# A state-space layer in a hybrid trunk: decay matrices in place, row copies by head group, rows requested two pairs ahead, first exponentials and first group's order tied

## The chip, the cores and the metric

The kernel runs on one core of one Trainium2 chip. The metric is the device time of one execution in microseconds. The program contains two layers of an encoder: three sub-layers each, of which one, the bidirectional state-space mixer, is touched by the change. Everything is computed in float32; the large projections split each operand into a high and a low part and use three products.

## The reference, cut to what matters

The mixer projects the 512 x 1024 input to z, x, B, C and dt, puts x, B and C through a short convolution and SiLU, and then runs one scan forward and one backward over 32 heads of 64 channels. Heads come in four groups of eight that share B and C (128 states). One direction is, chunk by chunk:

```python
a = (dt * A)                                   # per head and position
a_cs = cumsum(a)
L = exp(segsum(a))                             # decay from s to l, lower triangle
CB = einsum('bclgn,bcsgn->bgcls', Cc, Bc)      # shared by the heads of a group
y_diag = einsum('bgcls,bgjcls,bcsgjp->bclgjp', CB, L, Xc)
states = einsum('bclgn,bgjcl,bclgjp->bcgjpn', Bc, decay_states, Xc)
y_off = einsum('bclgn,bcgjpn,bgjcl->bclgjp', Cc, states, exp(a_cs))
y = y_f + y_b + X * d_skip                     # then SiLU(z), grouped RMS norm, w_out
```

So for each head there is a matrix of decays, exp(cumulated sum at l minus that at s), masked to a triangle, times C·B, times X. The kernel works with two chunks of 256 positions instead of four of 128.

## The kernel before, in words

**Who does what.** TensorE does projections, transposes and the products of the scan. ScalarE (ACT) does exponentials, SiLU, evictions of PSUM and the high halves of weights (L123). VectorE (DVE) does the low halves (L124), convolution taps (L743, L746), and elementwise products. GpSimd (POOL) masks the decay rows (L844) and adds the two masked halves (L858). All DMAs of this stage are asked for on SyncE's queue (SP), in one order.

**The rows.** `dt_chain` computes dt, the log decays and their cumulated sums, position on partitions, 64 columns for each of four blocks of 128 positions (32 heads forward, 32 backward). It transposes them (L720) to 64 rows of 512, one per head and direction, and evicts them as `rows` (L722) and, as exponentials, `rowe` (L724, L725). Four DMAs (L729) write both to DRAM as `scr`, 16 copies of every row, 3 MB together. A head's decay rows come back broadcast over 128 partitions: `rw` (forward and backward row, 512 KB, L827) and `ch` (exponential row, 256 KB, L829). Both are asked for in `ssd_head`, on demand, with two `rw` and three `ch` buffers.

**The matrices.** `ssd_head` multiplies ch by C (L830) and masks: two masks in place on rw, two into `dx`. `ssd_mats` makes, per head and chunk c, a matrix E (one of five buffers): two exponentials of 256 columns into E (L852, L853), two of 128 in dx (L854, L855), one add on GpSimd on the two diagonal blocks (L858), one product with C·B (`cb`) on VectorE (L859). The bias of each exponential is a column of `bias`, one per head. `ssd_out` then does the six products of a pair of heads (two heads side by side, 64 output rows each; L869): two with X transposed (`xt`), one with the carried state and ch.

**Groups and half pairs.** The loop at L929 goes over four groups, and within a group over eight steps s: four pairs of heads, two chunks each. A step is a half pair. Between the products of the steps stand the units of a list `todo`: projections of the next group's B, C and x (six units), of z, and, from the second group on, of the output. In the first group there are eight units. `prepare(g)` transposes B and x of a group, makes `cb`, and returns `sums`, which makes the carried states (L812, L816). At step 0 one unit runs first, and `sums` is kept behind it.

**What sets the order.** A planner takes the program in this order and, with its own costs, fixes for every engine one order of instructions ahead of the run; it may move a ready instruction ahead of one that it thinks is late. Extra edges can be given: `gated`/`shut` keep an instruction behind the last projection, and an edge without a semaphore (NOSYNC) sets only the order within an engine. The conv evictions of later units are already kept behind the last exponentials (`last_exp`, L741). Tiles of 128 x 512 come from one pool of 32 buffers (`big`); PSUM has four `acc`, two `mid` and two `ln` banks.

## Time and profile before

| what | value |
|---|---|
| median of 3 runs | 2158.78 us (2158.37 to 2164.72) |
| the profiled execution's own time | 2159.59 us |
| its span, first to last instruction | 2157.8 us |
| granted TensorE clock | 0.995 |
| TensorE matmul busy | 2111.7 us (98%) |
| VectorE busy | 1766.9 us (82%) |
| ScalarE busy | 1089.3 us (50%) |
| GpSimd busy | 165.0 us (8%) |
| state-space mixer, roughly | 380 to 790 us of the span |
| first group's scan in it, roughly | 439 to 506 us |

A row of the views gives an engine or a line of the kernel, what it writes from what, its count and its times in microseconds; behind an arrow stands what ended the idle time before it. Windows rows give a stretch, its length, and for each engine busy time and count in brackets; at the end stand the granted clock, the DMA engines' busy share and GB/s. Where such a row is filtered to one line of the kernel, only TensorE's two columns (products, weight loads) are left. SPq is SyncE issuing DMAs. A float32 product of the scan shows as two records.

### The profile page before, as it was taken

How to read it: one execution, taken by the hardware profiler on the slowest of the kernel's cores; microseconds unless marked ns; L12 is line 12 of the kernel's file. 1: busy time of each engine (PE TensorE's matmuls, PEld its weight loads, DVE VectorE, ACT ScalarE, POOL GpSimd, SP SyncE). 2: the span in 40 equal slices, each digit the busy share in tenths (PEclk: the TensorE clock that was granted, in tenths of full speed). 3: DMA queues.
4: the chain of work that ended last, by engine and by line, in shares of the span. 5: the costliest groups of instructions: out<-in, count | busy, mean ns of one | idle time of the engine just before them, and what ended most of it. 6: DMA issues, size and time to landing. Idle time of an engine off the chain costs nothing.

```text
span 2157.8 us, 34073 instructions
## 1 busy us (share of the span) xinstructions
PE 2111.7 (98%) x13230; PEld 1859.5 (86%) x13230; DVE 1766.9 (82%) x2924; ACT 1089.3 (50%) x1824; POOL 165.0 (8%) x258
## 2 busy tenths in 40 slices
PE   7999999999999999999999999999999999999997
PEld 6889899866777698999999989899888878989897
DVE  6979998557676888989988988997777878958796
ACT  4424354768656646344456434353866647424343
POOL 0000000045233400000000000000111100000000
PEclk9999999999999999999999999999999999999999
DMA  8863635375444442636443273723322212423231
GB/s 323 303 218 111 231 121 178 99 199 148 149 132 139 123 146 79 237 115 217 145 129 117 90 252 101 256 90 112 99 70 78 89 59 69 137 76 114 75 118 40
DMA packets 90082, 301.19 MB, mean 140 GB/s; under 512 B 10048, under 2 KB 13504, under 8 KB 89920
## 3 DMA queue, kind: packets, MB, share of 16 engines
q1 hardware_dynamic: 88384, 294.81, 41.7%
q0 software_dynamic: 1536, 4.20, 0.9%
q8 instruction: 104, 1.70, 0.3%
q14 instruction: 58, 0.48, 0.1%
HBM read 289.53 MB, written 5.24 MB: 137 GB/s over the span
## 4 chain that ended last, share of the span: by engine, by line
PE 84%; DVE 6%; issue 3%; ACT 3%; DMA 2%; POOL 2%; POOLq 0%; SPq 0%; ACTq 0%; DVEq 0%
PE acc L176 67%; PE mid L176 10%; PE mid L869 1%; DVE raw L195 1%; PE mid L1056 1%; DMA raw<-in_wdn 1%; PE ln L176 1%; POOL E L858 1%; DMA raw<-in_adaw 1%; DMA raw<-in_wgu 1%; ACT wh L123 1%; PE ln L1078 1%; DVE wl L124 1%; DVE wal L116 0%; PE ln L816 0%
## 5 line engine op out<-in xcount | busy, mean ns | idle before, releaser
L176 PE MATMUL acc<-hi,wh 128*128 128x256 f32 (+1 forms) x1568 | 522.1, 334 | 3.2 <-ACT hi L153 2.1
L176 PE MATMUL acc<-lo,wh 128*128 128x256 f32 (+1 forms) x1568 | 521.7, 333 | 0.3 <-DVE lo L154 0.2
L176 PE MATMUL acc<-hi,wl 128*128 128x256 f32 (+1 forms) x1568 | 522.0, 333 | 0.0
L176 PE MATMUL acc<-uh,wh 128*128 128x256 f32 (+1 forms) x1160 | 391.4, 338 | 0.1
L176 PE MATMUL acc<-ul,wh 128*128 128x256 f32 (+1 forms) x1160 | 389.8, 336 | 0.0
L176 PE MATMUL acc<-uh,wl 128*128 128x256 f32 (+1 forms) x1160 | 389.5, 336 | 0.0
L123 ACT ACTIVATE wh<-raw 128x1024 fp32r<-128x1024 f32 (+1 forms) x210 | 213.0, 1021 | 268.5 <-PE acc L176 103.1
L527 ACT ACTIVATE wh<-raw 128x1024 fp32r<-128x1024 f32 x198 | 209.3, 1059 | 250.0 <-DVE raw L537 117.5
L176 PEld LDWEIGHTS acc<-hi,wh 128*128 128x128 f32 x1568 | 296.1, 189 | 37.5 <-ACT hi L153 5.4
L176 PEld LDWEIGHTS acc<-lo,wh 128*128 128x128 f32 x1568 | 296.1, 189 | 30.5 <-DVE lo L154 2.1
L176 PEld LDWEIGHTS acc<-hi,wl 128*128 128x128 f32 x1568 | 296.1, 189 | 29.1
L124 DVE TENSOR_TENSOR wl<-raw,wh 128x1024 fp32r<-128x1024 f32 (+1 forms) x210 | 247.6, 1182 | 55.5 <-ACT wh L123 54.5
L528 DVE TENSOR_TENSOR wl<-raw,wh 128x1024 fp32r<-128x1024 f32 x198 | 241.0, 1219 | 22.0 <-ACT wh L527 21.1
L176 PEld LDWEIGHTS acc<-uh,wh 128*128 128x128 f32 x1160 | 219.4, 189 | 28.9 <-issue 5.9
L176 PEld LDWEIGHTS acc<-ul,wh 128*128 128x128 f32 x1160 | 219.8, 190 | 24.4 <-issue 2.8
L176 PEld LDWEIGHTS acc<-uh,wl 128*128 128x128 f32 x1160 | 219.8, 190 | 23.1 <-issue 1.5
L537 DVE TENSOR_TENSOR raw<-raw 128x512 f32<-128x512 f32 x264 | 181.3, 688 | 5.0 <-DMA raw<-in_wgu 0.2
L195 DVE SCALAR_TENSOR_TENSOR raw<-raw,cond 128x1024 f32<-128x1024 f32 x144 | 174.0, 1219 | 9.8 <-DMA raw<-in_adaw 9.4
L401 DVE SCALAR_TENSOR_TENSOR resid<-acc,gv,resid 128x512 f32<-128x512 f32 (+1 forms) x156 | 104.5, 672 | 69.3 <-PE acc L176 69.0
L341 POOL TENSOR_TENSOR rr<-vr,mhalf 128x2 f32<-128x2 f32 x12 | 9.2, 767 | 1516.5 <-DVE vr L337 1516.5
L176 PE MATMUL mid<-uh,wh 128*128 128x256 f32 (+2 forms) x332 | 99.7, 302 | 0.5 <-DVE up L569 0.5
L176 PE MATMUL mid<-uh,wl 128*128 128x256 f32 (+2 forms) x332 | 99.4, 299 | 0.0
(267 smaller groups left out, 3965.3 us busy)
## 6 DMA issues: line engine op xcount, KB each, us to landing
raw<-in_wgu SPq DMA_DIRECT2D x176, 512.0 KB, 4.0
raw<-in_adaw SPq DMA_DIRECT2D x144, 512.0 KB, 4.7
raw<-in_wdn SPq DMA_DIRECT2D x64, 448.0 KB, 4.0
raw<-in_win SPq DMA_DIRECT2D x40, 512.0 KB, 4.2
raw<-in_wdn SPq DMA_DIRECT2D x32, 512.0 KB, 4.7
rw<-scr SPq DMA_DIRECT2D x32, 512.0 KB, 5.6
ch<-scr SPq DMA_DIRECT2D x32, 256.0 KB, 3.7
raw<-in_wso SPq DMA_DIRECT2D x16, 512.0 KB, 3.6
```

The costliest lines, as they stand in the source:

```text
L123: nc.scalar.activation(hi[:, :n], raw, AF.Copy)
L124: nc.vector.tensor_tensor(out=lo[:, :n], in0=raw, in1=hi[:, :n].bitcast(F32), op=ALU.subtract)
L176: last = nc.tensor.matmul(o, lhsT=a, rhs=b, start=start and j == 0, stop=j == n - 1, skip_group_check=not start)
L195: nc.vector.scalar_tensor_tensor(out=raw, in0=raw, scalar=1.0, in1=cond, op0=ALU.mult, op1=ALU.mult, accum_out=mods[l][:, j : j + 1],)
L401: nc.vector.scalar_tensor_tensor(out=res[d][:, a:b], in0=pd[:, a:b], scalar=gvec[n][:, d : d + 1], in1=res[d][:, a:b], op0=ALU.mult, op1=A ...
L527: nc.scalar.activation(x[0], r, AF.Copy)
L528: nc.vector.tensor_tensor(out=x[1], in0=r, in1=x[0].bitcast(F32), op=ALU.subtract)
L537: nc.vector.tensor_tensor(out=o, in0=x, in1=y, op=ALU.add)
L858: nc.gpsimd.tensor_tensor(out=dg, in0=dg, in1=dx[:, c], op=ALU.add)
L869: nc.tensor.matmul(py[hh * 64 : (hh + 1) * 64, cc], lhsT=lhs, rhs=rhs, start=k == 0, stop=k == 2)
L1056: nc.tensor.matmul(ss[m], lhsT=q[:, c], rhs=qks[h, 1][m], start=j == 0, stop=j == 1)
L1078: gated(nc.tensor.transpose(pw[:, k * P : (k + 1) * P], w[:, k * P : (k + 1) * P], ident))
```

## The change

Heads are reordered in memory so that the eight heads of group g lie at rows g, g+4, ... of 32; `col(h)` finds a head's column. The exponentials are a third block of 32 rows, so one transpose gives 96 rows, and `rowe` goes. `scr` becomes four tensors, one per group, each written by three DMAs in `copy_rows`: group 0 at once, group g+1 at the second pair of group g. The E buffers go: the exponentials, the add and the product with C·B write over `rw`, of which there are six. `fetch` and `fetch_ch` ask for the rows of a pair two pairs ahead. The ch multiplication is done once for both heads. In the first group, the first pair's masks and the exponentials and matrices of its first half are put into `prepare`, between `cb` and `xt`, and the xt evictions are ordered behind the last of these exponentials. In the first group, too, the products of a half pair are kept behind the last projection (`shut`), the following projections behind the products (`hold`), and the units come two at a time after each pair. In all groups the first products of a half pair wait for both heads' matrices (`ready`).

```diff
+                if j == 0 and hold[0] is not None:
+                    tc.add_manual_dep(last.ins, hold[0].ins.name, NOSYNC, reason="behind the state-space products")
...
-        scr = dp.tile([16, 32, 3, T], F32, name="scr")
+        scr = [dp.tile([16, 8, 3, T], F32, name=f"scr{g}") for g in range(NG)]
+        rows = big(name="rows")
...
+            nc.vector.tensor_copy(cs[:, 0:2, 64:96], pc4[:, 0:2, 32:64])
+            nc.vector.tensor_copy(cs[:, 2:4, 64:96], pc4[:, 2:4, 0:32])
             pr = acc("ln")
             for i in range(4):
-                nc.tensor.transpose(pr[:64, i * P : (i + 1) * P], cs[:, i * 64 : (i + 1) * 64], ident)
-            rows = big(name="rows")
+                nc.tensor.transpose(pr[:96, i * P : (i + 1) * P], cs[:, i, :96], ident)
             nc.scalar.activation(rows[:64], pr[:64], AF.Copy)
-            rowe = big(name="rowe")
-            nc.scalar.activation(rowe[32:64, :W], pr[32:64, :W], AF.Exp)
-            nc.scalar.activation(rowe[0:32, W:], pr[0:32, W:], AF.Exp)
+            nc.scalar.activation(rows[64:96], pr[64:96], AF.Exp)
+            copy_rows(0)
...
-            for j, a, b, src in ((0, 0, T, rows[0:32]), (1, 0, T, rows[32:64]), (2, 0, W, rowe[32:64]), (2, W, T, rowe[0:32])):
-                nc.sync.dma_start(
-                    scr[:, :, j, a:b].rearrange("r h x -> h r x"), src[:, a:b].unsqueeze(1).broadcast_to([32, 16, b - a])
-                )
+        def copy_rows(g):
+            for j in range(3):
+                src = rows[j * 32 + g : j * 32 + 32 : 4].unsqueeze(1)
+                nc.sync.dma_start(scr[g][:, :, j].rearrange("r h x -> h r x"), src.broadcast_to([8, 16, T]))
...
+            first = between(cbs) if between else None
             for i in range(4):
...
-                nc.scalar.activation(x, pp, AF.Copy)
+                e = nc.scalar.activation(x, pp, AF.Copy)
+                if first is not None:
+                    tc.add_manual_dep(e.ins, first.ins.name, NOSYNC, reason="decay matrices first")
...
+        def fetch(ft):
+            if ft >= 16:
+                return
+            for h in (2 * ft, 2 * ft + 1):
+                rw = ep.tile([P, 2, T], F32, tag="rw", name="rw", bufs=NRW)
+                nc.sync.dma_start(rw, scr[h // 8][:, h % 8].unsqueeze(1)[:, :, 0:2].broadcast_to([NREP, P // NREP, 2, T]))
+                rows_of[h] = rw
...
+        def fetch_ch(ft):
+            if ft >= 16:
+                return
+            ch = ep.tile([P, 2, T], F32, tag="ch", name="ch")
+            for hh in range(2):
+                src = scr[ft // 4][:, 2 * ft % 8 + hh].unsqueeze(1)[:, :, 2]
+                nc.sync.dma_start(ch[:, hh, :], src.broadcast_to([NREP, P // NREP, T]))
+            ch_of[ft] = ch
+
+        def ssd_heads(ft, Ct):
+            ch = ch_of.pop(ft)
+            nc.vector.tensor_tensor(out=ch, in0=ch, in1=two(Ct), op=ALU.mult)
+            return [ssd_head(2 * ft + hh, ch[:, hh, :]) for hh in range(2)]
...
-            E = ep.tile([P, T], F32, tag="E", name="E", bufs=NE)
...
+            nc.scalar.activation(rw[:, 0, cc], rw[:, 0, cc], AF.Exp, bias=bias[:, i, col(h) : col(h) + 1])
+            nc.scalar.activation(rw[:, 1, cc], rw[:, 1, cc], AF.Exp, bias=bias[:, i + 1, 32 + col(h) : 33 + col(h)])
...
+            ready[c].append(
+                nc.vector.tensor_tensor(out=E, in0=E, in1=cbs[c].rearrange("p (k q) -> p k q", k=2), op=ALU.mult)
+            )
...
+                    m = gated(
+                        nc.tensor.matmul(py[hh * 64 : (hh + 1) * 64, cc], lhsT=lhs, rhs=rhs, start=k == 0, stop=k == 2)
+                    )
+                    for x in ready[c] if k == 0 else ():
+                        tc.add_manual_dep(m.ins, x.ins.name, SYNC, reason="one run of products")
...
+        for k in range(2):
+            fetch(k)
+            fetch_ch(k)
         silu(bc + xs)
...
+        def first_mats(cbs):
+            begun.extend(ssd_heads(0, bc[1]))
+            for hh in range(2):
+                ssd_mats(hh, 0, begun[hh][0], begun[hh][2], cbs)
+            return made[0]
+
+        cur = prepare(0, xs, bc, first_mats)
...
-                    heads = [ssd_head(ft * 2 + hh, Ct) for hh in range(2)]
+                    heads = begun if ft == 0 else ssd_heads(ft, Ct)
+                    if g < NG - 1 and pr_ == 1:
+                        copy_rows(g + 1)
                     py = acc("mid")
-                mats = [ssd_mats(ft * 2 + hh, c, heads[hh][0], heads[hh][2], cbs) for hh in range(2)]
+                for hh in range(2) if s or g else ():
+                    ssd_mats(ft * 2 + hh, c, heads[hh][0], heads[hh][2], cbs)
+                if c == 1:
+                    fetch(ft + 2)
...
-                ssd_out(pr_, c, py, mats, [hd[1] for hd in heads], xt, states)
+                if g == 0:
+                    shut()
+                last_out = ssd_out(pr_, c, heads, py, xt, states)
+                gate[0] = None
+                if c == 1:
+                    fetch_ch(ft + 2)
...
-                while done < (s + 1) * tot // 8:
+                if g == 0:
+                    hold[0] = last_out
+                while done < ((s + 1) // 2 * 2 if g == 0 else s + 1) * tot // 8 + (g == 0 and 0 < s < 7):
                     todo[done]()
                     done += 1
+                hold[0] = None
```

More of the change, by code (lines that the diff above doesn't have):

```diff
@@ L21 @@
 NA = 32
-NE = 5
+NRW = 6
 NG = 4
+NREP = 16
 NST = 128
@@ L160, in split_into @@
             )
-    last_mm, gate = [None], [None]
+    last_mm, gate, hold = [None], [None], [None]
     def gated(x):
@@ L678, in dt_chain @@
                 nc.tensor.transpose(pt[:, i * 64 : (i + 1) * 64], dtT[:64, i * P : (i + 1) * P], ident[:64, :64])
-            e1, e2, e3 = (ep.tile([P, T], F32, tag="E", name="E", bufs=NE) for _ in range(3))
+            e12, e3 = (ep.tile([P, 2, T], F32, tag="rw", name="ew", bufs=NRW) for _ in range(2))
+            e1, e2, e3 = e12[:, 0, :], e12[:, 1, :], e3[:, 0, :]
             v, q, e, uu, lu = e1[:, :W], e1[:, W:], e2[:, :W], e2[:, W:], e3[:, :W]
@@ L776, in silu, with prepare @@
                 tc.add_manual_dep(s.ins, last_in[0].ins.name, SYNC, reason="SiLUs together")
-        def prepare(g, xs, bc):
+        def prepare(g, xs, bc, between=None):
             Bt, Ct = bc
@@ L821, in prepare, with ssd_head @@
             return xt, cbs, states, Ct, sums
-        def ssd_head(h, Ct):
-            src = scr[:, h].unsqueeze(1)
-            rw = ep.tile([P, 2, T], F32, tag="rw", name="rw")
-            nc.sync.dma_start(rw, src[:, :, 0:2].broadcast_to([16, 8, 2, T]))
-            ch = ep.tile([P, T], F32, tag="ch", name="ch", bufs=3)
-            nc.sync.dma_start(ch, src[:, :, 2].broadcast_to([16, 8, T]))
-            nc.vector.tensor_tensor(out=ch, in0=ch, in1=Ct, op=ALU.mult)
+        rows_of = {}
+        def fetch(ft):
[5 more added lines that the diff above has]
+                rows_of[h] = rw
+        ch_of = {}
+        def fetch_ch(ft):
[10 more added lines that the diff above has]
+            return [ssd_head(2 * ft + hh, ch[:, hh, :]) for hh in range(2)]
+        def ssd_head(h, ch):
+            rw = rows_of.pop(h)
             dx = ep.tile([P, 2, 2, P], F32, tag="dx", name="dx")
@@ L849, in ssd_mats @@
         def ssd_mats(h, c, rw, dx, cbs):
[L850 to L855 removed]
+            i, cc = 2 * c, slice(c * W, (c + 1) * W)
@@ L858, in ssd_mats @@
+            dg = rw.rearrange("p d (k q) -> p (d k) q", k=4)[:, i : i + 6 : 5, :]
             nc.gpsimd.tensor_tensor(out=dg, in0=dg, in1=dx[:, c], op=ALU.add)
-            nc.vector.tensor_tensor(out=E, in0=E, in1=cbs[c], op=ALU.mult)
-            return E
-        def ssd_out(pr_, c, py, mats, chs, xt, states):
+            E = rw[:, :, cc]
+            ready[c].append(
+                nc.vector.tensor_tensor(out=E, in0=E, in1=cbs[c].rearrange("p (k q) -> p k q", k=2), op=ALU.mult)
+            )
@@ L863, in ssd_out @@
+        def ssd_out(pr_, c, heads, py, xt, states):
+            col = [slice(pr_ * P + hh * 64, pr_ * P + (hh + 1) * 64) for hh in range(2)]
             cc = slice(c * W, (c + 1) * W)
-            col = [slice(pr_ * P + hh * 64, pr_ * P + (hh + 1) * 64) for hh in range(2)]
             for k in range(3):
                 for hh in range(2):
+                    rw, ch, _ = heads[hh]
                     lhs = xt[2 * c + k][:, col[hh]] if k < 2 else states[1 - c][:, col[hh]]
-                    rhs = mats[hh][:, k * W : (k + 1) * W] if k < 2 else chs[hh][:, cc]
-                    nc.tensor.matmul(py[hh * 64 : (hh + 1) * 64, cc], lhsT=lhs, rhs=rhs, start=k == 0, stop=k == 2)
+                    rhs = rw[:, k, cc] if k < 2 else ch[:, cc]
+                    m = gated(
+                        nc.tensor.matmul(py[hh * 64 : (hh + 1) * 64, cc], lhsT=lhs, rhs=rhs, start=k == 0, stop=k == 2)
+                    )
+                    for x in ready[c] if k == 0 else ():
+                        tc.add_manual_dep(m.ins, x.ins.name, SYNC, reason="one run of products")
+            ready[c].clear()
+            return m
@@ L871, in gated_norm @@
+        ready = [[], []]
         def gated_norm(g, ys, zs, fill=None):
@@ L917, in ssm @@
         run(units_z(0, zs[0])[:2])
-        cur = prepare(0, xs, bc)
+        begun = []
+        def first_mats(cbs):
[4 more added lines that the diff above has]
+        cur = prepare(0, xs, bc, first_mats)
         outs, yrs = {}, {}
@@ L1228, in _layout @@
     A["par"] = par
+    heads = np.arange(32).reshape(4, 8).T.reshape(-1)
+    heads = np.concatenate([heads, heads + 32])
     A["dtp"] = cc(np.concatenate(
-        [rows(np.tile(f[k][0].reshape(-1), 4)) for k in ("ssm_dt_bias", "ssm_a_log")], axis=1
+        [rows(np.tile(f[k][0].reshape(-1)[heads], 4)) for k in ("ssm_dt_bias", "ssm_a_log")], axis=1
     ))
@@ L1256, in _layout @@
     w = f["ssm_w_in"][0]
-    A["wdt"] = cc(w[:, 5120:].reshape(KT, P, 64).transpose(1, 0, 2).reshape(P, 512))
+    A["wdt"] = cc(w[:, 5120:][:, heads].reshape(KT, P, 64).transpose(1, 0, 2).reshape(P, 512))
     b = unit(w[:, :5120])
```

23 lines of the change are left out of this document (12 added, 11 removed).

## The prediction

> **What bounds the kernel now.** I read the page first, then the chain of waits through the state-space layer, then TensorE's own work in stretches of it.
>
> ```profile
> span 2157.8 us, 34073 instructions
> PE 84%; DVE 6%; issue 3%; ACT 3%; DMA 2%; POOL 2%; POOLq 0%; SPq 0%; ACTq 0%; DVEq 0%
> ```
>
> TensorE carries 84% of the chain, so a saving must show as a shorter stretch of TensorE. A busy TensorE proves little: its records overlap, and a product that waits inside the queue still looks busy. So I count instructions. The next rows are the chain in the second head group, where nothing disturbs it.
>
> ```profile
> 532.72 10.93 PE acc L176 x48
> 543.66 1.45 PE mid L869 x12
> ```
>
> Two projections of 24 products are 48 in 10.93 us; the twelve records of one half pair (L869, the state-space products) are 1.45 us, 0.121 each. Now the same two lines over three stretches (length; busy time and count): the first group's from its third half pair's projections on, the quiet one, and the last group's end. The first three rows are L176, the last three L869.
>
> ```profile
> 461.71:506.19 44.48, 30.61 (x119) 21.62 (x119) 1.00 0.76 213
> 532.48:588.33 55.85, 50.35 (x216) 40.13 (x216) 1.00 0.49 151
> 721.49:740.68 19.19, 11.48 (x48) 8.85 (x48) 1.00 0.47 124
> ```
>
> ```profile
> 461.71:506.19 44.48, 12.94 (x74) 5.70 (x72) 1.00 0.76 213
> 532.48:588.33 55.85, 6.06 (x48) 3.09 (x48) 1.00 0.49 151
> 721.49:740.68 19.19, 4.93 (x38) 2.58 (x36) 1.00 0.47 124
> ```
>
> The quiet stretch prices a projection product, the change-overs included: (55.85 - 48 x 0.121) / 216 = 0.232 us. By that the first group's stretch should take 119 x 0.232 + 74 x 0.121 = 36.5 us and takes 44.48: **8.0 us lost**. The last group's end should take 48 x 0.232 + 36 x 0.121 = 15.5 and takes 19.19: **3.7 us lost**. These two are the prize. The clock is 1.00 in all of them, so the loss is order and waits. The chain in the first group shows which:
>
> ```profile
> 442.70 16.33 PE acc L176 x72
> 459.04 2.77 PE mid L869 x24
> 461.80 3.19 DMA ch<-scr
> ...
> 466.75 0.65 PE mid L869 x2
> 467.40 1.13 PE acc L176 x4
> 468.53 1.47 PE mid L869 x10
> ```
>
> Three projections run, then the first pair unbroken. From the second pair on, one head's first product goes out alone (x2), four projection products fall between, then the other ten: the pair is broken up, and the chain goes back to a row transfer before it. GpSimd says how far apart the pairs are (in-place masks, L844, first of each pair):
>
> ```profile
> 473.36 1.14 POOL L844 TENSOR_SCALAR_AFFINE_SELECT rw<-rw 128x256 f32<-128x256 f32 x2 [6.08 <-DMA rw<-scr]
> 483.96 0.77 POOL L844 TENSOR_SCALAR_AFFINE_SELECT rw<-rw 128x256 f32<-128x256 f32 x2 [2.22 <-DMA rw<-scr]
> 494.68 0.80 POOL L844 TENSOR_SCALAR_AFFINE_SELECT rw<-rw 128x256 f32<-128x256 f32 x2 [2.17 <-DMA rw<-scr]
> ```
>
> From 473.36 to 483.96 to 494.68 a pair takes 10.6 and 10.7 us, 2.2 of them waiting for the transfer: about 8.5 us of masks, exponentials, adds and products with C·B per pair.
>
> **Part 1: first group's order fixed (hold, gate, ready).** It adds no instruction; it makes TensorE run two projections, then both half pairs of a pair unbroken, and so on. A pair then needs 10.93 + 2 x 1.45 = 13.8 us of TensorE. The matrices need 8.5 (transfer hidden) to 10.6, so they stay ahead, and the 8.0 us should come back. The bounds are 0 (every pair just late) and 8.0. I take 7.5, near the upper end, because the measured 10.6, wait included, is already below 13.8. The new wait sits on TensorE: behind the first product of a half pair stand all later projections, and behind those ScalarE's conv evictions. The cover is the two projections ahead of each pair.
>
> **Part 2: rows asked for two pairs ahead, matrices in place (NRW = 6, no E).** It removes the five E buffers; the exponentials write over the rows, so the first now waits for all four masks of its head instead of two. Same number of masks, exponentials, adds and products. The multiplication of ch is one instruction of 1024 columns instead of two of 512, on VectorE, hidden. Bytes read back stay the same: 32 times 512 KB and 32 times 256 KB. What moves is the request, past weight loads on SP's queue. What it is worth shows in the last group:
>
> ```profile
> 722.91 1.20 SPq L827 DMA_DIRECT2D rw<-scr  x2
> ...
> 728.55 2.75 POOL L844 TENSOR_SCALAR_AFFINE_SELECT rw<-rw 128x256 f32<-128x256 f32 x2 [3.98 <-DMA rw<-scr]
> ...
> 737.60 0.62 PE L869 MATMUL mid<-E,xt 128*64 128x256 f32 x2 [1.73 <-DVE E L859]
> 739.24 0.86 PE L869 MATMUL mid<-E,xt 128*64 128x256 f32 x5 [1.03 <-DVE E L859]
> ```
>
> The last pair's rows are asked for at 722.91, GpSimd idles 3.98 us for them, and TensorE then waits at 737.60 and 739.24. Asked for two pairs earlier they are there: the masks start some 4 us sooner, which covers 3 of the 3.7 us (between 0, if VectorE is late instead, and 3.7). I take 3.0, and 0.5 more for the last group's first half, whose masks wait the same way. What is late next there is VectorE, whose row stands with the rivals. `fetch_ch` waits for the pair's products and stands on SP ahead of weight loads; the old kernel's ch requests waited there too, and four raw buffers cover it: nothing.
>
> **Part 3: 96 rows, copies per group.** The old four copies move 3 MB before the first pair may be read; the new first three move 0.79 MB (3 x 8 heads x 16 copies x 2 KB), the rest follow one group at a time (nine more issues on SP, well ahead of use: nothing). Two small VectorE copies and one table-free eviction less on the way; the nearest VectorE row is below, 0.29, so +0.6 at most, on a chain that TensorE covers with projections.
>
> ```profile
> 410.78 0.29 DVE L697 TENSOR_SCALAR E<-E 128x256 f32<-128x256 f32 x1
> 416.93 0.86 SPq L729 DMA_DIRECT2D scr<-rows  x2
> 417.84 4.64 SPq L729 DMA_DIRECT2D scr<-rowe  x2
> 429.07 3.00 SPq L827 DMA_DIRECT2D rw<-scr  x2
> 437.93 0.78 POOL L844 TENSOR_SCALAR_AFFINE_SELECT rw<-rw 128x256 f32<-128x256 f32 x2 [59.12 <-issue]
> ```
>
> ```profile
> 418.00:433.00 15.00, 14.98 (x73) 12.11 (x71) 7.96 (x10) 10.67 (x16) 0.00 (x0) 1.00 0.99 194
> 435.00:441.00 6.00, 6.00 (x24) 4.31 (x23) 1.60 (x3) 2.00 (x3) 2.13 (x5) 1.00 1.03 243
> ```
>
> The next row is the landing time of the 256 KB ch requests:
>
> ```profile
> DMA to landing us min/median/max: 3.1/3.7/7.2
> ```
>
> The transfers were the limit there: 99% of the engines at 194 GB/s while the copies ran, 243 while rows came back. At 194 the two parts that the first rows need (0.52 MB) take 2.7 us, and a landing has some 2 us on top of its bytes (an estimate: 3.1 for 256 KB, less 1.1 at 243 GB/s). So the request goes out near 423 (417.3 when the rows are ready, 0.7 for the issues, 2.7, 2) instead of 429.07; two rows of 0.52 MB at 243 take 4.3, and 2 to land. I expect the two heads' rows at 427 and 430, against 437.93 for the first before. The far bound is that nothing is won: 438.
>
> A rule speaks against this. By the Trainium skill ("DMA: Bandwidth & Descriptors", section "Why a DMA increments its semaphore by 16 and not by 1") a DMA uses the largest number of engines up to 16 that divides the outermost size of both its sides; the new copies have 8 heads outermost, so 8 engines. The old ones, 32 outermost, agree (99% busy); no run here shows one with 8. By it the sum would be some 2.5 us worse.
>
> **Part 4: first exponentials tied early.** The first pair's masks and first eight exponentials move ahead of the four xt evictions, which now wait for the last of them.
>
> ```profile
> 431.81 0.60 ACT L796 ACTIVATE cb<-ln 128x512 f32<-128x512 f32 x1 [0.63 <-PE ln L791]
> 434.49 0.60 ACT L803 ACTIVATE xt<-ln 128x512 f32<-128x512 f32 x1 [0.26 <-PE ln L801]
> 440.15 1.28 ACT L852 ACT_TABLE_LOAD   x1
> 443.94 0.39 ACT L855 ACTIVATE dx<-dx,ssbias 128x128 f32<-128x128 f32 x1
> 439.11 3.59 PE L816 MATMUL ln<-xd,bt 128*128 128x512 f32 x8
> ```
>
> Before: xt out by 435.1, the state sums on TensorE at 439.11, the table load at 440.15 and eight exponentials done at 444.3, 4.2 us in all. After: they follow the cb evictions, 432.4 + 4.2 = 436.6, then xt until about 439. Behind the wait are the xt evictions, the transposes that need their banks, and the sums: these slip from 439.1 to some 439.5. More costly is the new order: before, three projections ran between the sums and the first products (442.70 to 459.04 in the chain's rows, 72 products); now both half pairs must run first, and the second half's exponentials come only after xt, ready near 444, when TensorE is there. I take **+2**. The bounds are 0 (all in time) and +8 (rows at 438, eight exponentials by 444, xt by 446.5, sums 7 to 8 us late).
>
> **Sum**, from the profiled execution's 2159.59: -7.5 - 3.0 - 0.5 + 2.0 = -9.0, so 2150.6. The median of the runs is 0.8 below that execution: **2149.8, say 2150**. Own range 2145.5 to 2153.5 (start 0 to 4, first group 6 to 8, last group 1 to 4). A difference below 0.3% (6.5 us) can't be told from no change.
>
> **Rivals.**
>
> *Everything comes back* (10%): start 0, 8.0 and 3.7, and the rest of the last group's waits: about 2145. For it: the 8.5 us against 13.8. Against: GpSimd's masks at times take three times their usual length (2.75 us for two at 728.55, 0.78 at 437.93).
>
> *Late start* (17%): the small first copies don't run at full rate. At half of 194, 0.79 MB takes 8 us and the two needed parts 5.4, rows at 430 to 434, sums 3 to 5 us late; with the upper bound of +8 the gain is 11 - 8 = 3 us. Time 2153 to 2156. For it: the old copies kept the transfers full for 15 us, and a rows request must wait for a landing. Against: a quarter of the bytes. The skill's eight-engine rule named above is this case in its mild form.
>
> *Given back on VectorE* (6%): the last group cannot shrink, because VectorE is the next bound.
>
> ```profile
> 701.85:740.68 38.83, 33.80 (x178) 21.86 (x176) 31.41 (x39) 24.88 (x53) 22.14 (x28) 1.00 0.47 129
> ```
>
> VectorE (the third busy time) works 31.41 of 38.83 us there; 3.5 us less makes it 89% busy, in order. Then only the first group's gain is left, less some: 2153 to 2155.
>
> *Slower* (12%): the tie at the start. Eight exponentials stand before xt, the sums and every later product, and the fixed order forbids projections to fill the hole. Every microsecond that the first rows land after about 431 is a microsecond of idle TensorE. The other terms give 11, so it decides once the rows land after 442: 5 us later than before, for instance if the copies' requests and the two pairs' 3 MB queue ahead of each other. At 448 it costs 17 less 11: 2165. Against it: the bytes ahead of the first rows fall from 3 MB to 0.5 MB.
>
> That the change doesn't do what it says (the planner already had a pair's products together) is excluded for the first group's later pairs by the x2 and x10 rows.
>
> **How the numbers follow.** Forecast 55%, the rivals 10, 17, 6 and 12. Faster by over 0.3% means below 2152.3: 50 of the forecast's 55, the 10, and 2 of the late start: 0.62. Slower: 0.12. The rest, 0.26, is within. The range 2144 to 2160 leaves out the slower case and little at the fast end.
>
> **What would show it.** In the changed profile: L869 in unbroken runs of 24 in the first group, with two projections (48 products) between; the first group's masks not waiting for rows; the first masks near 430 instead of 437.93; the state sums (L816) of the first group within 2 us of 439.1; the last pair's wait of TensorE for VectorE gone; the second group's first transposes some 5 us before 506.19. It is wrong if TensorE waits for exponentials before each pair of the first group, if the sums start after 443, or if the last group keeps its waits.

## The result: slower by 0.6%

The changed kernel takes 2173.89 us (median of 4 runs, 2171.77 to 2176.05), the kernel before 2160.44 (4 runs, 2158.37 to 2164.72; the three runs known ahead had 2158.78): a ratio of 1.0063, 95% interval 1.005 to 1.0075. It is 13.5 us **slower**, where some 9 us of gain were forecast. The profiled execution took 2176.05 us, its span is 16.5 us longer than before. In the experiments below three executions at a granted clock of 0.65 to 0.84, the traced one of exp_and_ch among them, took 2310 to 2980 us and are left out of every ratio. These are the span and the chain's shares on the page of the profile after:

```profile
span 2174.3 us, 34054 instructions
PE 80%; DVE 10%; ACT 3%; DMA 3%; issue 2%; POOL 1%; SPq 0%; POOLq 0%; ACTq 0%; DVEq 0%
```

TensorE's share of the chain is down from 84 to 80%: other engines now hold it up. Where the time is lost shows when landmarks of TensorE's order are set side by side. The first transposes of the second, third and fourth group (L795) and the norm's broadcast (L267), in TensorE's timeline of the profile after:

```profile
518.66 0.66 PE L795 MATMUL ln<-csts,xc 128*128 128x128 f32 x4
...
606.67 0.60 PE L795 MATMUL ln<-csts,xc 128*128 128x128 f32 x4
...
704.84 0.60 PE L795 MATMUL ln<-csts,xc 128*128 128x128 f32 x4
...
780.32 0.65 PE L267 MATMUL ln<-csts,rr 128*128 128x128 f32 x4 [3.12 <-POOL rr L261]
```

| landmark | before | after | behind by |
|---|---|---|---|
| first group's state sums | 439.11 | 446.07 | 7.0 |
| second group's first transposes | 506.19 | 518.66 | 12.5 |
| third group's | 588.33 | 606.67 | 18.3 |
| fourth group's | 685.13 | 704.84 | 19.7 |
| last half pair's products | 746.35 | 760.90 | 14.5 |
| norm's broadcast | 762.50 | 780.32 | 17.8 |
| span | 2157.8 | 2174.3 | 16.5 |

Up to the transposes of the decay rows the two traces agree (415.23 and 415.39), so the table shows the change. The first two groups lose 18, the last group gains 5 as it should, and 3 of these go again at the norm. Four places, read one by one.

**The start.** GpSimd's first masks (L880), each head's:

```profile
427.07 0.78 POOL L880 TENSOR_SCALAR_AFFINE_SELECT rw<-rw 128x256 f32<-128x256 f32 x2 [47.69 <-issue]
...
429.11 1.75 POOL L880 TENSOR_SCALAR_AFFINE_SELECT rw<-rw 128x256 f32<-128x256 f32 x2 [0.53 <-DMA rw<-scr]
```

The rows are there at 427 and 429, ten us earlier than before; each head has two such rows of masks, and the last is over at 431.6. But ScalarE does this in the meantime:

```profile
430.87 0.60 ACT L808 ACTIVATE cb<-ln 128x512 f32<-128x512 f32 x1 [0.62 <-PE ln L803]
437.03 1.06 ACT L124 ACTIVATE wh<-raw 128x1024 fp32r<-128x1024 f32 x1 [5.56 <-PE acc L177]
438.11 1.28 ACT L888 ACT_TABLE_LOAD   x1
439.40 0.51 ACT L888 ACTIVATE rw<-rw,ssbias 128x256 f32<-128x256 f32 x1
...
441.89 0.39 ACT L890 ACTIVATE dx<-dx,ssbias 128x128 f32<-128x128 f32 x1
442.18 1.06 ACT L816 ACTIVATE xt<-ln 128x512 f32<-128x512 f32 x2
```

Between cb and the exponentials stands the split of a weight unit (L124). It needs one of three weight buffers, and that is free only when TensorE has finished the projection that runs just then: 5.56 us of waiting with masked rows behind it. The tie then puts xt behind the exponentials, and TensorE runs dry:

```profile
442.81 1.97 PE L814 MATMUL ln<-csts,xc 128*128 128x128 f32 x8 [5.59 <-ACT xt L816]
...
446.07 4.63 PE L831 MATMUL ln<-xd,bt 128*128 128x512 f32 x8
...
453.59 0.65 PE L909 MATMUL mid<-ch,st 128*64 128x256 f32 x4 [1.88 <-ACT st L833]
```

**The first group.** TensorE's products of the projections (L177) and of the scan (L909), from the first pair to the second group's transposes, then in the second group, then at the last group's end:

```profile
455.47:518.66 63.19, 47.44 (x190) 36.88 (x190) 0.92 0.63 179
544.86:606.67 61.81, 51.94 (x216) 41.33 (x216) 0.97 0.55 168
738.50:762.34 23.84, 17.24 (x72) 13.28 (x72) 1.00 0.29 89
```

```profile
455.47:518.66 63.19, 8.50 (x74) 4.90 (x72) 0.92 0.63 179
544.86:606.67 61.81, 6.06 (x48) 3.09 (x48) 0.97 0.55 168
738.50:762.34 23.84, 6.79 (x58) 3.60 (x54) 1.00 0.29 89
```

By the prediction's prices the first stretch should take 190 x 0.232 + 74 x 0.121 = 53.0 us and takes 63.2: 10.2 lost, more than the 8.0 before. The second, quiet before, loses 5.9. The third loses 0.6 (with the 54 records that start in it; four of the 58 began ahead of it) against 3.7: the last group's gain is there. What is lost in the first group is lost at one place, in the second pair of units, whose 48 products take 21.99 us (469.31 to 491.30), 10.9 over their price:

```profile
481.04 0.80 PE L177 MATMUL acc<-uh,wh 128*128 128x512 f32 x1 [5.95 <-ACT wh L124]
...
484.04 0.80 PE L177 MATMUL acc<-uh,wl 128*128 128x512 f32 x1 [1.78 <-DVE wl L125]
...
485.06 0.63 PE L177 MATMUL acc<-ul,wh 128*128 128x512 f32 x1
485.49 0.63 PE L177 MATMUL acc<-uh,wl 128*128 128x512 f32 x1
```

TensorE waits for the high half of a weight unit, then for the low half. That unit was asked for late, on SP, and split late, on ScalarE:

```profile
469.42 1.16 SPq L856 DMA_DIRECT2D ch<-scr  x2
470.63 0.58 SPq L100 DMA_DIRECT2D raw<-in_win  x1
```

```profile
475.13 0.78 ACT L752 ACTIVATE xc<-acc,pars 128x512 f32<-128x512 f32 x1 [7.67 <-PE acc L177]
475.80 0.49 ACT L888 ACTIVATE rw<-rw,ssbias 128x256 f32<-128x256 f32 x1
...
479.95 1.04 ACT L124 ACTIVATE wh<-raw 128x1024 fp32r<-128x1024 f32 x1
```

On SP the load stands behind a ch request that waits for a pair's products; on ScalarE the split stands behind the convolution's eviction of the unit before (which waits 7.67 us for TensorE to end that unit) and behind twelve exponentials that nobody needs yet.

**The last group and the norm.** The scan's products in the last group, grouped, have no wait left:

```profile
L909 PE MATMUL mid<-rw,xt 128*64 128x256 f32 x64 | 9.2, 388 | 0.0
```

The same view of before:

```profile
L869 PE MATMUL mid<-E,xt 128*64 128x256 f32 x64 | 9.8, 389 | 4.1 <-DVE E L859 4.1
```

Behind the last bar stand the idle time and what ended it: 4.1 us of waiting for VectorE are gone. But at the norm TensorE waits 3.12 us for GpSimd's rr (in the first fence), which it didn't before. VectorE's timeline ahead of it, of before and then of after:

```profile
759.81 0.16 DVE L256 TENSOR_SCALAR rv<-ln 128x4 f32<-128x4 f32 x1
759.94 1.23 DVE L124 TENSOR_TENSOR wl<-raw,wh 128x1024 fp32r<-128x1024 f32 x1
```

```profile
776.30 1.23 DVE L125 TENSOR_TENSOR wl<-raw,wh 128x1024 fp32r<-128x1024 f32 x1 [2.16 <-ACT wh L124]
777.45 0.74 DVE L404 SCALAR_TENSOR_TENSOR resid<-acc,gv,resid 128x512 f32<-128x512 f32 x1
778.11 0.15 DVE L259 TENSOR_SCALAR rv<-ln 128x4 f32<-128x4 f32 x1
```

The short rv stood ahead of the weight split; in the changed kernel's order it stands behind one that waits.

### The profile page after: what moved, and what is told of

It is laid out like the page before. It is cut to its first block, busy times and chain, and to the rows that moved or that the text cites. A ratio compares the mean times of both kernels' runs of the same rounds, so it can differ in the third digit from the quotient of the medians.

```text
span 2174.3 us, 34054 instructions
## 1 busy us (share of the span) xinstructions
PE 2112.5 (97%) x13230; PEld 1861.1 (86%) x13230; DVE 1763.6 (81%) x2910; ACT 1086.4 (50%) x1823; POOL 165.8 (8%) x258
## 4 chain that ended last, share of the span: by engine, by line
PE 80%; DVE 10%; ACT 3%; DMA 3%; issue 2%; POOL 1%; SPq 0%; POOLq 0%; ACTq 0%; DVEq 0%
PE acc L177 65%; PE mid L177 9%; PE mid L909 1%; DVE wl L125 1%; DVE raw L198 1%; PE mid L1127 1%; DMA raw<-in_wdn 1%; PE ln L177 1%; DVE raw L540 1%; DVE wl L531 1%; DMA raw<-in_wso 1%; ACT wh L124 1%; DMA raw<-in_adaw 1%; DVE rw L897 1%; DVE lo L155 1%
## 5 line engine op out<-in xcount | busy, mean ns | idle before, releaser
L177 PE MATMUL acc<-hi,wh 128*128 128x256 f32 (+1 forms) x1568 | 521.9, 334 | 2.9 <-ACT hi L154 1.8
L177 PE MATMUL acc<-lo,wh 128*128 128x256 f32 (+1 forms) x1568 | 521.5, 333 | 0.4 <-DVE lo L155 0.2
L177 PE MATMUL acc<-hi,wl 128*128 128x256 f32 (+1 forms) x1568 | 521.7, 333 | 0.0
L177 PE MATMUL acc<-uh,wh 128*128 128x256 f32 (+1 forms) x1160 | 392.2, 339 | 7.7 <-ACT wh L124 7.7
L177 PE MATMUL acc<-uh,wl 128*128 128x256 f32 (+1 forms) x1160 | 390.3, 337 | 4.0 <-DVE wl L125 4.0
L177 PE MATMUL acc<-ul,wh 128*128 128x256 f32 (+1 forms) x1160 | 390.5, 337 | 0.5 <-DVE ul L1245 0.5
L124 ACT ACTIVATE wh<-raw 128x1024 fp32r<-128x1024 f32 (+1 forms) x210 | 212.7, 1021 | 265.4 <-DMA raw<-in_wdn 99.7
L177 PEld LDWEIGHTS acc<-hi,wh 128*128 128x128 f32 x1568 | 295.9, 189 | 36.9 <-ACT hi L154 4.6
L177 PEld LDWEIGHTS acc<-lo,wh 128*128 128x128 f32 x1568 | 296.1, 189 | 30.5 <-DVE lo L155 2.1
L177 PEld LDWEIGHTS acc<-hi,wl 128*128 128x128 f32 x1568 | 296.1, 189 | 29.1
L177 PEld LDWEIGHTS acc<-uh,wh 128*128 128x128 f32 x1160 | 220.2, 190 | 36.8 <-ACT wh L124 8.9
L177 PEld LDWEIGHTS acc<-uh,wl 128*128 128x128 f32 x1160 | 220.4, 190 | 27.3 <-DVE wl L125 5.2
L177 PEld LDWEIGHTS acc<-ul,wh 128*128 128x128 f32 x1160 | 220.6, 190 | 23.4 <-DVE ul L1245 1.0
L198 DVE SCALAR_TENSOR_TENSOR raw<-raw,cond 128x1024 f32<-128x1024 f32 x144 | 173.9, 1219 | 10.6 <-DMA raw<-in_adaw 10.2
L177 PE MATMUL mid<-uh,wh 128*128 128x256 f32 (+2 forms) x332 | 99.9, 302 | 1.1 <-DVE up L572 0.9
L177 PE MATMUL mid<-uh,wl 128*128 128x256 f32 (+2 forms) x332 | 99.3, 299 | 0.0
```

Source lines behind the costliest of these rows:

```text
L124: nc.scalar.activation(hi[:, :n], raw, AF.Copy)
L177: last = nc.tensor.matmul(o, lhsT=a, rhs=b, start=start and j == 0, stop=j == n - 1, skip_group_check=not start)
L198: nc.vector.scalar_tensor_tensor(out=raw, in0=raw, scalar=1.0, in1=cond, op0=ALU.mult, op1=ALU.mult, accum_out=mods[l][:, j : j + 1],)
```

## The experiments

Ratios are to the kernel before, run on the same chip (medians 2157.97, 2159.14, 2158.64 and 2158.98 in the four sets); "against the changed kernel" compares ratios, taken times 2159 us, since it was itself run in a set of its own.

| run | ratio, 95% interval | against the changed kernel |
|---|---|---|
| the change | 1.0063 (1.005 to 1.0075) | |
| exp_first | 1.0040 (1.0026 to 1.0053) | -5.0 |
| untied | 1.0063 (1.0043 to 1.0082) | 0 |
| ch_after | 1.0048 (1.0029 to 1.0068) | -3.2 |
| free_order | 1.0045 (1.0029 to 1.006) | -3.9 |
| early | 1.0020 (1.001 to 1.003) | -9.3 |
| early_exp | 1.0004 (0.9992 to 1.0015) | -12.7 |
| exp_and_ch | 1.0024 (1.0014 to 1.0033) | -8.4 |
| parts23 | 1.0011 (1.0001 to 1.002) | -11.2 |
| norm_first | 1.0068 (1.0056 to 1.008) | +1.1 |
| fill_first | 1.0037 (1.0024 to 1.005) | -5.6 |
| all_mended | 1.0030 (1.002 to 1.0041) | -7.1 |
| next_group | 1.0002 (0.9993 to 1.0011) | -13.2 |

**exp_first: the weight split behind the first exponentials.**

```diff
-        nc.scalar.activation(hi[:, :n], raw, AF.Copy)
+        x = nc.scalar.activation(hi[:, :n], raw, AF.Copy)
+        if wait_exp[0] is not None:
+            tc.add_manual_dep(x.ins, wait_exp[0].ins.name, NOSYNC, reason="weights behind the first exponentials")
...
+                    wait_exp[0] = made[0] if g == 0 else None
```

> The changed kernel, with the weight splits of the first group's later units ordered behind the first pair's first eight exponentials on ScalarE. Theory 1 (a weight split that waits for TensorE's unit 0 stands ahead of the exponentials): the exponentials begin near 432 instead of 439, the state sums near 441 instead of 446, and some 5 to 7 us of the start's loss come back: about 2167 against 2174. Rival 1 (the tie of xt to the exponentials costs wherever they start): nothing changes, 2172 to 2175.

2167.44 us, as theory 1 expected. The table load moves from 438.11 to 434.06, the sums from 446.07 to 441.58. TensorE's sums of this run:

```profile
441.58 2.84 PE L833 MATMUL ln<-xd,bt 128*128 128x512 f32 x6
445.55 1.13 PE L833 MATMUL ln<-xd,bt 128*128 128x512 f32 x2 [1.13 <-DVE xd L829]
```

So the split's place is most of the start's loss. Counted from the transposes of the rows (416.60 here, 415.23 before), the sums now start 1.1 us later than before, and 1.13 us of waiting stand among them: about the prediction's +2. The second place stays as it was: 5.96 and 1.77 us for the weights.

**untied: xt no longer behind the exponentials.**

```diff
-                if first is not None:
-                    tc.add_manual_dep(e.ins, first.ins.name, NOSYNC, reason="decay matrices first")
```

> The changed kernel without the edge that keeps the xt evictions behind the first exponentials. Theory 1: the sums start near 439 as before, but the split still stands ahead of the exponentials, which still begin near 439, so the first products wait and only 3 to 5 us come back, about 2170. Rival 1: the start's loss of about 10 us goes nearly whole, about 2164.

2173.14 us, no difference; the theory had about 2170 and the rival 2164, so both are missed. The sums start at 437.99 and then the products wait, 3.92 us here and 3.05 at the second half pair:

```profile
437.99 3.59 PE L829 MATMUL ln<-xd,bt 128*128 128x512 f32 x8
445.51 1.42 PE L907 MATMUL mid<-rw,xt 128*64 128x256 f32 x8 [3.92 <-DVE rw L895]
```

The tie only chooses who waits. The exponentials are late in both kernels, because of the split ahead of them, and the fixed order gives TensorE nothing else to do.

**ch_after: the ch requests behind the step's weight loads.**

```diff
-                    fetch_ch(ft + 2)
-                if c == 1:
...
                 hold[0] = None
+                if c == 1:
+                    fetch_ch(ft + 2)
```

> The changed kernel, with the ch requests of a pair written behind the units of that step, so that unit 4's weights are asked for ahead of pair 3's ch. Theory 2 (a ch request that waits for a pair's products stands ahead of weight loads on SP): unit 4's load goes out near 457 instead of 470.6, TensorE's waits of 5.95 and 1.78 us for weights in the first group are gone, and with them the slow products behind them: 9 to 11 us, about 2164. Rival 2 (the forced order asks for the weights too late, whatever SP does): the waits stay, 2172 to 2175.

2169.87 us, between the two expectations (2164, and 2172 to 2175). The load goes out at 461.53 instead of 470.63, and the split starts at 479.55 instead of 479.95: ScalarE, not the load, held it. The wait for wh falls only from 5.95 to 4.39 us, the one for wl goes. In the second group the wait for weights at 549.21 goes, and the pair waits 4.44 us for ch at 550.73 instead: there SP's order is the cause, and both orders cost something.

**free_order: the first group's order left to the planner** (shut and hold taken out for the first group, units spread over half pairs again).

```diff
-                if g == 0:
-                    shut()
...
-                if g == 0:
-                    hold[0] = last_out
-                while done < ((s + 1) // 2 * 2 if g == 0 else s + 1) * tot // 8 + (g == 0 and 0 < s < 7):
+                while done < (s + 1) * tot // 8:
```

> The changed kernel without the forced order of the first group: no products kept behind projections, no projections kept behind products, one unit per half pair as in the kernel before. Theory 2: the ch requests still stand ahead of weight loads, so weights are still late, but a free TensorE order fills the hole at the start with a projection: 2166 to 2171. Rival 2: the weights come in time, the start is filled, 2160 to 2163.

2169.04 us, within the theory's expectation: the fixed order alone is not the loss either. Without it the sums come at 456.39, and the products behind them are broken up by waits for st, rw and ch of 1.7 to 2.5 us each and by two of 2.1 and 4.5 us for which the trace names no engine.

**early: a step's weight units written ahead of its exponentials** (first group only).

```diff
+                if g == 0:
+                    for j in {1: (11, 12), 3: (13, 14), 5: (15, 8), 7: (9,)}.get(s, ()):
+                        split_of[j] = split(load(win[j]))
                 for hh in range(2) if s or g else ():
                     ssd_mats(ft * 2 + hh, c, heads[hh][0], heads[hh][2], cbs)
```

> The edit: in the first group the two weight units of a step (load, split on ScalarE, rest on VectorE) are written ahead of that step's exponentials; nothing else of the changed kernel is touched, so the weight split ahead of the first exponentials stays and so does the late start. Theory (ScalarE's order: the split of a weight unit stands behind the convolution's eviction and a pair's exponentials, and TensorE waits for it): the waits for wh and wl between 469 and 491 (10.9 us over the quiet price) fall to under 4 us, the span by 6 to 9 us, 2162 to 2166. Rival (the splits only change places with the exponentials): the waits come back ahead of the products as waits for rw, the loss stays within 3 us of what it was, 2168 to 2173.

2163.52 us, 9.3 less than the change: within the theory's expectation. The same place in TensorE's timeline:

```profile
479.74 0.50 PE L177 MATMUL acc<-uh,wh 128*128 128x512 f32 x1 [1.81 <-ACT wh L124]
...
481.50 0.75 PE L177 MATMUL acc<-uh,wl 128*128 128x512 f32 x1 [1.02 <-DVE wl L125]
```

Its 48 products take 16.14 us instead of 21.99, 5.0 over the price instead of 10.9. The expectation had under 4: the named waits are 2.8, but by the loss over the price, from which it started, it is missed. Writing the units early moves both links of the delay: the load goes out at 461.13 instead of 470.63, as in ch_after, and the split now also stands ahead of the exponentials; the split moved without the load was not run. What is left has the same form: the split now starts at 478.64, right behind the convolution's eviction at 477.97 that waits 7.67 us for TensorE to end the unit before.

**early_exp: both.**

> The edit: the weight units of a step ahead of its exponentials, and the first weight splits held behind the first half pair's exponentials; both of ScalarE's late places mended, the fixed order, the tie and the rows two pairs ahead all kept. Theory (the whole loss is these two places): state sums near 441.5, the waits for wh and wl under 4 us, 2157 to 2162, about the kernel before. Rival (the fixed order leaves no slack, so a mended wait opens the next one): 2164 to 2168, with the loss in the first group still over 10 us and another name behind the waits.

2160.52 us, the kernel before within the measurement, and within the theory's expectation. The two edits give 5.0 and 9.3 alone and 12.7 of the 13.5 together. So **mending these two places, where a weight split stands wrongly in ScalarE's order or its load wrongly in SP's, takes back the slowdown**, with the fixed order, the tie and the rows two pairs ahead all still in. It doesn't bring the forecast's gain: in this trace the third group's first transposes stand at 598.23, still 9.9 behind the kernel before, and the norm's broadcast at 766.61, 4.1 behind: the later groups only make up for part of what the first two lose. One thing that it still loses, at the start:

```profile
449.81 1.97 PE L916 MATMUL mid<-rw,xt 128*64 128x256 f32 x8 [3.94 <-DVE rw L904]
```

The second half of the first pair is 3.94 us late, with projections at hand that may not run. The prediction's Part 4 had named this order, but had the second half's exponentials ready in time ("near 444, when TensorE is there").

**exp_and_ch: exp_first and ch_after together.**

> The edit: the first weight splits held behind the first half pair's exponentials, and the requests of ch moved behind the step's weight units. Alone, the first took 6.4 us off the changed kernel's median and the second 4.0. If the two mend different losses they add: 2162 to 2165, with unit 4's load near 458 and the wait for wh under 5 us. If the load's place on SP is not what holds the split (ScalarE's order is), nothing is added: 2166 to 2169, the wait for wh at 5 to 6 us as with the first alone.

2163.13 us: 8.4 less, against 5.0 + 3.2. As far as the intervals tell, they add. The trace of this run isn't read.

**parts23: no fixed order and no tie** (the edits of free_order and untied together; the rows two pairs ahead, the matrices in place and the copies by group are left).

> The edit: the fixed order of the first group and the edge that puts the xt evictions behind the first exponentials are both taken out; what is left of the change is the rows two pairs ahead, the matrices in place and the copies per group. The prediction put these at 3.5 us gained. If the whole loss lies in the order and the tie: 2153 to 2157 and the first group's loss no more than before. If the parts that are left carry it (the ch requests on SP ahead of weight loads, the weight split ahead of the first exponentials): 2164 to 2170, with broken products in the first group as with the order alone taken out (2169).

2161.91 us, neither of the two expectations: the parts that were forecast to gain 3.5 us gain nothing, but they don't carry the loss. The last group does gain: from its sums to its last products it takes 39.17 us (708.68 to 747.85) instead of 44.50 (701.85 to 746.35). But the first group, from its sums to the second group's first transposes, takes 74.24 (439.08 to 513.32) instead of 67.08, and TensorE waits 2.41 us for rr at the norm.

11.2 of the 13.5 us are gone in this run, and the weight split still stands ahead of the first exponentials, as it does in the kernel before:

```profile
439.06 1.06 ACT L124 ACTIVATE wh<-raw 128x1024 fp32r<-128x1024 f32 x1 [3.97 <-PE acc L177]
```

TensorE doesn't feel it here: the sums start at 439.08 and projections run until the first products at 458.94. So the loss at the start needs both, a split that stands wrongly, and an order and a tie that leave TensorE nothing else to do; taking away either mends most of it.

**norm_first: the norm's rv ahead of the last two units' weight splits** (their VectorE halves; order only), on the changed kernel.

```diff
+        if wait_rv[0] is not None:
+            tc.add_manual_dep(y.ins, wait_rv[0].ins.name, NOSYNC, reason="weights behind the norm")
...
+        wait_rv[0] = last_rv[0]
         send(tail, yr)
+        wait_rv[0] = None
```

> The edit, on the changed kernel: in the last group the weight splits of the following units stand behind the norm's small VectorE instruction (rv) and no longer ahead of it; nothing in the first group is touched. In the changed kernel TensorE waits 3.12 us for GpSimd's rr there, which the kernel before does not; rr waits for rv, and rv stands behind a weight split and a residual addition on VectorE. Theory (a third place of one kind: a split that waits stands ahead of a short instruction that TensorE needs): the wait for rr goes, 2 to 3 us less, 2168.5 to 2170 against some 2171.5 for the changed kernel on this chip. Rival (rv is late for its own data, or the displaced splits are late in their turn): the wait stays or comes back as one for wl behind the norm, no change, 2171 to 2172.5.

In the trace the wait goes, as the theory says: rv starts at 774.38, rr at 774.62, and the norm's broadcast stands 3.68 us behind its sums instead of 6.95.

```profile
773.39 0.95 PE L935 MATMUL ln<-invg,gss 128*128 128x1 f32 x8
...
777.07 0.60 PE L270 MATMUL ln<-csts,rr 128*128 128x128 f32 x4
```

The times don't confirm it: 2172.58 us (2169.91 to 2177.06), ratio 1.0068, expected 2168.5 to 2170. The intervals of the ratios just leave room for 3 us. That mending the place shortens the kernel is not shown. Nor is 3 us its steady price: in exp_first's trace the same rows stand in the same order (a split that waits 1.87 us ahead of rv), and TensorE waits 0.29 us for rr; in early's it waits 2.16.

**fill_first: one unit between the sums and the first products**, on early_exp.

```diff
                     sums()
                     gate[0] = None
+                    if g == 0:
+                        todo[1]()
+                        done = 2
```

> The edit, on the kernel with both of ScalarE's late places mended (2160.5): one projection unit of the first group (24 products, 5.5 us) stands between the state sums and the first pair's products, as in the kernel before, instead of behind the first pair; all other order is kept. There TensorE waited 3.94 us for the first pair's matrices (rw, VectorE) with projections at hand that the fixed order forbade. Theory (the fixed order's price at the start is the missing filler): that wait goes, the start loses under 2 us, 3 to 5 us less, 2155 to 2158. Rival (the unit's weights are late in turn, or the gain is absorbed by the weight wait of the next pairs, 6.1 us there): 2159 to 2161.

2167.3 us: **worse** than early_exp by 7, outside both expectations. The wait for rw at the start is gone, and those for weights are larger, 3.99 us for the high half and 2.69 for the low (1.81 and 1.02 in early_exp):

```profile
466.62 0.50 PE L179 MATMUL acc<-uh,wh 128*128 128x512 f32 x1 [3.99 <-ACT wh L124]
```

In the second group the wait for wh is 3.22 us, at the norm the one for rr 1.95. Its last products stand 2.1 us behind early_exp's and the norm adds 1.6; some 3 us of the difference are not located.

**all_mended and next_group: is there a version below both?** The first joins fill_first and norm_first; the second takes early_exp, norm_first and, in the second group, the units of two half pairs written early.

> The edits of the two runs beside it together: both late places of ScalarE mended, one unit between the sums and the first products, and the weight splits behind the norm's small instruction in the last group. If each place costs what its trace showed and they add: 2152 to 2156, below both kernels (ratio to the kernel before 0.997 to 0.999). If the change's own gain in the last group is already eaten elsewhere: 2157 to 2160, no difference from the kernel before.

```diff
+                if g == 1:
+                    for j in {1: (21, 22), 2: (23, 24)}.get(s, ()):
+                        split_of[j] = split(load(win[j]))
```

> The edits, on the kernel with both late places of ScalarE mended (2160.5, no unit moved): the norm's small instruction ahead of the weight splits in the last group, and in the second group the weight units of the second and third half pair written ahead of their exponentials, as in the first group. Its trace had 3.1 us lost to weights in the second group and 0.3 us of wait for rr. If each mended place counts by its trace: 2156 to 2158.5, at or a little below the kernel before (0.998 to 0.9995). If a mended place is paid for by the next (as the moved unit was): 2159 to 2163.

2165.15 us and 2159.38. All_mended misses both its expectations: it inherits fill_first's waits (4.32 and 2.34 us for weights), and its interval overlaps with fill_first's. Next_group equals the kernel before (0.9993 to 1.0011) and lies in the second of its two expectations. Its edit in the second group moved nothing there: TensorE still waits 1.28 and 1.86 us for the weights, because on SP the loads (538.31) stand behind the ch request (537.06) as they did. No version that was run is faster than the kernel before.

## Why the prediction was wrong

**Part 4 is the first step that failed**: "After: they follow the cb evictions, 432.4 + 4.2 = 436.6". They followed a weight split and were done at 442.3. The +2 became 7.0 by the sums' landmark; exp_first, with the split put behind, takes 5.0 off the time and leaves about the +2. The upper bound of +8 held, but for another reason: it was made from rows that land late, and they landed at 427 and 429, as Part 3 had them (427 and 430). The split could have been seen: in the kernel before, this row of ScalarE stands right ahead of the table load that the prediction quotes at 440.15.

```profile
439.08 1.06 ACT L123 ACTIVATE wh<-raw 128x1024 fp32r<-128x1024 f32 x1 [3.99 <-PE acc L176]
440.15 1.28 ACT L852 ACT_TABLE_LOAD   x1
```

The exponentials were read as late because rows were late (437.93). They were also behind a split that waits for TensorE, and the rows' gain of 10 us could not pass it.

**Part 2, second failing step**: "`fetch_ch` waits for the pair's products and stands on SP ahead of weight loads; the old kernel's ch requests waited there too, and four raw buffers cover it: nothing". It named the queue and priced it at nothing. The wait for weights that it belongs to costs 10.9 us in the first group, and 4.0 us of named waits in the second (1.74 and 2.25). With the load put right alone (ch_after) 3.2 us come back and the split is still at 479.55; with load and split put right (early) 9.3. **Part 1** is wrong with it, and is the largest miss: from the sums to the second group's first transposes the kernel loses 5.5 us (12.5 less 7.0) where 7.5 were to be gained. Its mechanism is right: the first group's products go out unbroken, 24 with 48 projection products between, in the second to fourth pair TensorE never waits for matrices, and outside the 48 products that wait for weights the stretch loses nothing (10.2 less 10.9). But its price, -7.5, set the matrices (8.5 to 10.6 us) against TensorE's 13.8 and left out the weights: the cover was "the two projections ahead of each pair", and the second of these two was itself not ready. The step had listed ScalarE's convolution evictions as queued behind; that weight splits queue behind these was the next link, and it was not followed. No part priced the second group, which loses 5.8 (18.3 less 12.5): 4.0 of it are the named waits for weights, the rest stays open.

**Part 2's gain was right** in place and a little small: 3.0 + 0.5 in the last group; the landmarks show 19.7 - 14.5 = 5.2, the lost time 3.1 at its end. The question "what is late next" was answered with VectorE's load; what came was VectorE's order, 3.1 us at the norm in this trace, a stage later.

**Part 3 was right**, and the rule weighed there held in what it says of engines and not in the price worked out from it. The first three copies in the profile after (windows of 1 us, the last two numbers are the DMA engines' share and GB/s):

```profile
419.00:420.00 1.00, 1.00 (x7) 0.81 (x6) 1.00 (x3) 0.98 (x2) 0.00 (x0) 1.00 0.52 199
420.00:421.00 1.00, 1.00 (x6) 0.84 (x5) 1.00 (x3) 1.00 (x1) 0.00 (x0) 1.00 0.53 164
```

By the Trainium skill ("DMA: Bandwidth & Descriptors", section "Why a DMA increments its semaphore by 16 and not by 1") eight heads outermost take eight engines; the share of about one half agrees. But half the engines moved 164 to 199 GB/s, and all sixteen moved 194 before. The 2.5 us that would have been lost were not.

**The rivals.** "Slower" had the sign at 12%, by a mechanism that didn't happen (rows after 442), and 2165; its sentence that the fixed order "forbids projections to fill the hole" is what made the late exponentials dear. "Late start" and "given back on VectorE" named places that did lose, by other mechanisms. One slip had no effect: the forecast's own bounds for its parts add up to 2147 to 2156, not to 2145.5 to 2153.5. The parts were costed one by one against the trace of before, and no rival looked at where the weight splits stand. The first stood in the same place in the kernel before; the change ties xt, and so TensorE, to the exponentials that follow it. The other two are new: the change gave the planner a new program, and it set one split behind twelve exponentials and one ahead of rv.

## What to carry to other kernels

Before moving an instruction earlier on an in-order engine, read the row directly ahead of it there and what that one waits for; an earlier input is worth nothing behind a neighbour that waits. When a fixed order takes filler work away from the busiest engine, price every input of what is left, weights and their buffers too, and not just the input that the change is about. A gain in one stage can go again in the next, where a short instruction stands behind one that waits; a trace shows it here, no measured time does.

## What the runs showed of the hardware

Long waits cost more than their length. TensorE's windows in the profile after, around the two waits (the first number behind the counts in brackets is the granted clock):

```profile
443.00:446.00 3.00, 2.75 (x10) 1.66 (x9) 2.38 (x4) 3.00 (x8) 3.00 (x4) 0.50 0.00 0
446.00:450.00 4.00, 4.00 (x8) 1.70 (x8) 4.00 (x5) 3.07 (x9) 3.93 (x6) 0.82 0.00 0
...
481.00:485.00 4.00, 2.18 (x4) 1.33 (x5) 2.99 (x3) 2.08 (x6) 4.00 (x6) 0.50 0.69 266
485.00:488.00 3.00, 3.00 (x8) 2.31 (x7) 0.87 (x1) 1.94 (x6) 2.91 (x6) 0.50 0.55 171
488.00:492.00 4.00, 4.00 (x21) 2.88 (x21) 2.45 (x2) 4.00 (x9) 1.23 (x1) 0.95 0.14 29
```

After 5.6 and 6 us of idling the clock is 0.50. After the first wait (work from 442.81) it is back within the window from 446, after the second (work from 481.04, with 1.78 us of waiting in between) only in the one from 488. While it is 0.50, products start every 0.43 us (485.06, 485.49) where 48 in 10.93 make 0.228. In the first group 7.7 us of named waits became 10.9 us of loss. The Trainium skill ("TensorE: Matmul & The Clock Gate", section "What's actually happening") gives half clock after an idle window of some 3.4 us and full clock after as long of work; the half clock agrees, and the way back took longer here, about 5 and 7 us (worked out from the 0.82 and 0.95 of the last windows). Before, the windows of the first group show 1.00: of the 8.0 us that it lost by the prediction's prices the trace names only 2.2 as waits (0.40, 0.35 and 1.42 us), all short. So the clock stayed up in the broken order and fell in the one long wait of the unbroken order.
